# Attention outputs leave one step later: copies and adds moved behind the next split in a hybrid encoder layer

## The chip, the cores and the metric

The kernel runs on one core of one Trainium2 chip. The metric is the device time in microseconds of one launch, as the median of several runs; lower is better. The core has five engines with a queue each: TensorE (PE, with its weight loads as PEld), VectorE (DVE), ScalarE (ACT), GpSimd (POOL) and SyncE (SP), which only issues transfers here. An engine takes the instructions of its queue in order. Engines meet through semaphores.

## The reference

One layer over 1024 tokens of 1024 features, all in float32:

```python
hn = rmsnorm(h, norm_mix)
proj = einsum('bsd,de->bse', hn, w_in)           # 2304 columns: qa, ka, va, qb, kb, vb
o_a = window_gqa_sink(qa, ka, va, sink)          # 8 heads, 2 key heads, |i-j| <= 128, rotary on 16 of 64 dims
o_b = neighbourhood_attention(qb, kb, vb, rpb)   # 8 heads on a 16 x 64 grid, window 8 x 16, learned bias
mix = concatenate([rmsnorm(o_a, norm_a), rmsnorm(o_b, norm_b)])
h = h + einsum('bse,ed->bsd', mix, w_out)
hn = rmsnorm(h, norm_ffn)
h = h + down(silu(conv3(gate(hn))) * up(hn))     # 2816 inner features
return rmsnorm(h, norm_final)
```

Both attentions are softmax(scores) times values; the first has one extra logit per head (the sink) in its denominator.

## The kernel before, in words

Features lie on the 128 partitions and tokens along the free dimension. Every float32 product is made of three matmuls in a reduced format: each operand is split into a high part (a rounded copy) and a low part (the rest), and high by high, low by high and high by low are accumulated. ScalarE makes the high part, VectorE subtracts to get the low one.

The kernel has three stages: the first projections, then attention interleaved with the other projections (about 60 to 350 us), then the gated MLP. The second stage matters here. It is a list of units. A window unit (`unit_window`) is one block of 128 queries of a group of four heads; a grid unit (`units_grid`) is a part of one head's eight blocks. A unit has two kinds of steps:

- a q step makes scores (PE L393), reduces and biases them on VectorE (L424), takes the exponential on ScalarE (L432) and, for a pair, the reciprocal of the sums on VectorE (L434) and the scaling on GpSimd (L436).
- a t step transposes the scaled probabilities into a PSUM bank `pt` (PE L472 for windows, L548 for the grid) and splits them in `split_pt`: the high part `ph` on ScalarE (L446), the low part `pl` on VectorE (L447). The marks "high" and "rest" name the latest of these two. The t step returns a v step.
- a v step multiplies values with `ph` and `pl` into the output bank `o` (PE L478 and L479, grid L559 and L560). It is issued one t step later, so that the split has time.

When the last v step of a unit (of a half head on the grid) has been issued, `leave` takes the output out of `o`. The output lies in two halves of partitions, one product with the high and one with the low half of the values, and they have to be added across partitions: ScalarE copies one half into `ot` (L491, grid L574), VectorE adds the other half and writes it to `mix` (L495, grid L576). There is one `ot` buffer and there are two `o` banks.

Between these steps a generator (`rest`) fills TensorE with the remaining projections, three matmuls at a time (L179, L180, L181) into one of two banks `pj`, at rates set by the table `RATES`. The last of these jobs (`OutA`) are the first half of the output projection; each adds its bank to the residual on VectorE (L659) and so frees it. Projections of queries, keys and values leave their bank at L242 or L247.

TensorE's order is the order in which the code is written. On the other engines a scheduler sets the order by priority (`tc.high_priority`) and dependences. `behind(*names)` puts what is traced inside it behind the marked instructions of the same engine's queue; it orders the queue and adds no wait on a semaphore. The page's names are those of the code: `s` scores, `nm` the negated maximum, `sm` the sums, `xr` the residual's input, `raw`, `whi` and `wlo` a weight and its parts.

Of the kernel before, what the change touches and what calls it, by code (L numbers as in the profile page):

```python
# [58 lines left out]
def hybrid_layer(tc, xT, w_first, w_in, w_out, w_gate, w_up, w_down, small, sink, rpb, consts, rope, out):  # L59
    nc = tc.nc  # L60
    with ExitStack() as ctx:
# [13 lines left out]
        def big(name, tag, dt=F32):  # L75
            return lpool.tile([128, S], dt, name=name, tag=tag, bufs=slots[tag])
# [77 lines left out]
        def behind(*names):  # L154

            stack = ExitStack()
            for n in names:
                stack.enter_context(tc.issue_after(mark[n].ins))
            return stack
# [242 lines left out]
                return lpool.tile([128, 2, 386], F32, name="p", tag="mix", bufs=slots["mix"], padded_shape=[128, 2, 512])  # L402
            return apool.tile([128, 2, 386], F32, name="p", tag="p", bufs=5, padded_shape=[128, 2, 392])

        deferred = []

        def exponentials(*order):
            while deferred:
                with tc.high_priority(offset=50):
                    deferred.pop(0)(*order)  # L410
# [31 lines left out]
        def split_pt(ps, n):  # L442
            ph = apool.tile([128, HALF], F32R, name="ph", tag="ph")
            pl = apool.tile([128, HALF], F32R, name="pl", tag="pl")
            with tc.high_priority(offset=100):
                mark["high"] = nc.scalar.activation(ph[:, 0:n], ps[:, 0:n], AF.Copy)  # L446
                mark["rest"] = nc.vector.tensor_tensor(pl[:, 0:n], ps[:, 0:n], f32(ph[:, 0:n]), op=ALU.subtract)  # L447
            return ph, pl

        def unit_window(g, b):  # L450

            cs, n = near(b), 128 * len(near(b))
            ps4 = [None] * 4
            mask = w2(cst[:, K_MA + 128 * (cs[0] - b + 1):K_MA + 128 * (cs[-1] - b + 2)])
            st = {}

            def q_step(j):
                def go():
                    if j % 2 == 0:
                        st["p"] = pair_tile(True)  # L460
                    ps, _ = scores(qa[g, j // 2][j % 2], ka[g], b)
                    softmax(st, j % 2, ps, n, mask, nsink[:, 4 * g + j - j % 2:4 * g + j - j % 2 + 2])
                    ps4[j] = st["p"][:, j % 2, :]
                return go

            def t_step(i):
                def go():
                    if i == 0:
                        st["o"] = bank("o", "o")
                    pt = bank("pt", "pt")  # L470
                    for j in range(4):
                        nc.tensor.transpose(pt[:, j * 128:(j + 1) * 128], ps4[j][:, i * 128:(i + 1) * 128], ident)  # L472
                    ph, pl = split_pt(pt, HALF)
                    exponentials("high")

                    def v_step():
                        o, v = st["o"], va[g]
                        nc.tensor.matmul(o, v[:, cs[i], :], mv(ph[:, :]), start=i == 0, stop=False)  # L478
                        nc.tensor.matmul(o, v[:, cs[i], :], mv(pl[:, :]), start=False, stop=i == len(cs) - 1)  # L479
                        if i == len(cs) - 1:  # L480
                            leave()
                    return v_step
                return go

            def leave():
                ot = apool.tile([128, 2, 128], F32, name="ot", tag="ot", bufs=1, padded_shape=[128, 4, 128])
                o4 = pv(st["o"][:, :])
                halved = lambda ap: ap.rearrange("p (s w) -> p s w", s=2)
                for e in range(2):
                    me, other = slice(64 * e, 64 * e + 64), slice(64 - 64 * e, 128 - 64 * e)  # L490
                    nc.scalar.activation(ot[me].rearrange("p j (s w) -> p j s w", s=2), o4[other, e::2], AF.Copy)  # L491
                    for i in range(2):
                        if mix[2 * g + i] is None:
                            mix[2 * g + i] = big("mixa", "mix")
                        nc.vector.tensor_tensor(halved(mix[2 * g + i][me, b * 128:(b + 1) * 128]), o4[me, e + 2 * i], halved(ot[me, i, :]), op=ALU.add)  # L495

            return [q_step(j) for j in range(4)], [t_step(i) for i in range(len(cs))]

# [19 lines left out]
        def units_grid(h):  # L518

            ps4 = [None] * NB  # L520
            st = {"begun": [False, False]}
            e = 64 * (h % 2)
            me, other = slice(e, e + 64), slice(64 - e, 128 - e)

            def q_step(b):
                def go():
                    if b == 0:
                        bias_of[h] = bias_of.pop(h, None) or bias_tiles(h)
                    if b == 4 and h < 7:
                        bias_of[h + 1] = bias_tiles(h + 1)  # L530
                    x = bias_of[h]
                    if b % 2 == 0:
                        st["p"] = pair_tile()
                    sel = slice(2, 5, 2) if b == 0 else slice(0, 3, 2) if b == NB - 1 else slice(1, 4)
                    ps, n = scores(qb[h], kb[h], b)
                    softmax(st, b % 2, ps, n, x[:, sel, :] if n == 256 else w2(x[:, sel, :].rearrange("p c w -> p (c w)")))
                    ps4[b] = st["p"][:, b % 2, :]
                return go

            def t_step(c):  # L540
                def go():
                    if c == 0:
                        st["o"] = [bank("o", "o") for _ in range(2)]
                    bs = near(c)
                    pt = bank("pt", "pt")
                    for i, b in enumerate(bs):
                        at = near(b).index(c) * 128
                        nc.tensor.transpose(pt[:, i * 128:(i + 1) * 128], ps4[b][:, at:at + 128], ident)  # L548
                    ph, pl = split_pt(pt, 128 * len(bs))

                    def v_step():
                        for half in range(2):
                            inb = [b for b in bs if b // 4 == half]
                            if not inb:
                                continue
                            lo, hi = (inb[0] - bs[0]) * 128, (inb[-1] - bs[0] + 1) * 128
                            dst = st["o"][half][:, (inb[0] % 4) * 128:(inb[-1] % 4 + 1) * 128]
                            final = c == (4 if half == 0 else NB - 1)
                            nc.tensor.matmul(dst, vb[h][:, c, :], mv(ph[:, lo:hi]), start=not st["begun"][half], stop=False, skip_group_check=True)  # L559
                            nc.tensor.matmul(dst, vb[h][:, c, :], mv(pl[:, lo:hi]), start=False, stop=final, skip_group_check=True)  # L560
                            st["begun"][half] = True
                            if final:
                                leave(half)
                    return v_step
                return go

            def leave(half):
                i = 4 + h // 2
                if mix[i] is None:
                    mix[i] = big("mixb", "mix")  # L570
                ot = apool.tile([128, HALF], F32, name="ot", tag="ot", bufs=1)
                w = lambda ap: ap.rearrange("p (b r c s) -> p b s r c", s=2, r=ROWS // 2, c=8)
                o = st["o"][half]
                nc.scalar.activation(ot[me], o[other], AF.Copy)  # L574
                dst = mix[i][me, :].rearrange("p (s r b c) -> p b s r c", s=2, b=NB, c=8)[:, 4 * half:4 * half + 4]
                nc.vector.tensor_tensor(dst, w(o[me, :]), w(ot[me, :]), op=ALU.add)  # L576

            chunks = [[0], [1, 2], [3, 4], [5, 6, 7]]
            return [([q_step(2 * i), q_step(2 * i + 1)], [t_step(c) for c in chunks[i]]) for i in range(4)]
# [56 lines left out]
        class OutA:  # L636
# [12 lines left out]
            def run(self):  # L649
                d = self.d  # L650
                h1[d] = big("h1", "mix" if d < 4 else "op")
                xt = tmp("xr")
                with behind(*["stacked"] * (d > 0)):
                    nc.sync.dma_start(xt, xT[d])
                for h in range(2):
                    ps = bank("pj", "pj")
                    yield from product(ps, self.w, mg[0:4], h)
                    with tc.high_priority(offset=500):
                        nc.vector.tensor_tensor(sv(h1[d][:, tsl(h)]), pv(ps[:, :]), sv(xt[:, tsl(h)]), op=ALU.add)  # L659

            def post(self):
# [304 lines left out]
            nc.scalar.activation(warm, eps, AF.Sqrt)  # L966
        fill(2)
        pend()


        last = tmp("sq")
# [712 lines left out]
```

## Time and profile before

| | us |
|---|---|
| median of 3 runs | 1016.34 |
| lowest and highest run | 1015.89, 1016.55 |
| the profiled execution, whole | 1016.91 |
| its span, first to last instruction | 1015.1 |
| TensorE busy | 1006.3 |
| VectorE busy | 832.7 |
| ScalarE busy | 561.8 |
| GpSimd busy | 104.0 |

In the rows of the timeline the first number is the start in us from the start of the span, the second the time to the end of the row's last instruction, then engine, line, operation, what is written and read, the shape, and how many instructions the row merges; a bracket gives the idle time of the engine before it and what ended it. In the list of waits the numbers are the total in us, how many waits, and the longest. A matmul's end is modelled, and matmuls overlap; what TensorE loses at a place is read from the distances between starts. A row of the instruction order has the line, the operation, what is written and read with buffer numbers, and the shape; it has no time in it.

### The profile page before, as it was taken

To read this page: it belongs to the slowest core of one execution; us is meant where nothing else is said; L and a number is where in the kernel's file an instruction comes from. 1 tells how busy PE (TensorE), PEld (TensorE's weight loads), DVE (VectorE), ACT (ScalarE), POOL (GpSimd) and SP (SyncE) were. 2 spreads that over 40 slices of the span, in tenths; PEclk is the share of its full clock that TensorE was granted. 3 is DMA by queue.
4 is the path that set the end of the run, shared out by engine and by line. 5 is a ranking of instruction groups with operands and counts; after the bars stand their busy time and mean duration, and the time that the engine had idled before them with its cause. 6 is when DMAs were issued, how large, how long until landed. Compare 5 with 4: busy or idle time off the path is not lost.

```text
span 1015.1 us, 14835 instructions
## 1 busy us (share of the span) xinstructions
PE 1006.3 (99%) x5086; PEld 890.2 (88%) x5086; DVE 832.7 (82%) x1566; ACT 561.8 (55%) x1081; POOL 104.0 (10%) x188
## 2 busy tenths in 40 slices
PE   9999999999999999999999999999999999999996
PEld 8899898899899888888888888888888888888886
DVE  7989887768888799999987786786777678986775
ACT  8567776658687554565544443444443645544451
POOL 0224342222232100000000000000000000000002
PEclk9999999999999999999999999999999999999999
DMA  8223122333334366231542233323232699866644
GB/s 295 83 74 92 34 73 63 83 83 83 84 93 135 126 203 222 73 104 63 203 180 100 98 115 114 104 94 131 88 135 88 227 345 322 297 226 231 226 153 166
DMA packets 68220, 144.94 MB, mean 143 GB/s; under 512 B 8240, under 2 KB 18736, under 8 KB 68144
## 3 DMA queue, kind: packets, MB, share of 16 engines
q1 hardware_dynamic: 58208, 118.88, 36.5%
q10 hardware_dynamic: 9936, 25.11, 6.4%
q8 instruction: 40, 0.66, 0.3%
q14 instruction: 36, 0.29, 0.1%
HBM read 103.58 MB, written 28.57 MB: 130 GB/s over the span
## 4 chain that ended last, share of the span: by engine, by line
PE 99%; DVE 1%; issue 0%; ACT 0%; DVEq 0%; POOL 0%; POOLq 0%
PE pj L179 8%; PE pj L181 8%; PE pj L180 8%; PE x L1045 7%; PE x L1043 7%; PE x L1044 7%; PE dn L1045 7%; PE dn L1044 7%; PE dn L1043 7%; PE s L393 4%; PE y L1045 4%; PE y L1043 4%; PE y L1044 4%; PE pt L472 2%; PE z L1043 2%; PE z L1045 2%
## 5 line engine op out<-in xcount | busy, mean ns | idle before, releaser
L1043 PE MATMUL x<-hg,whi 128*128 128x512 f32 x352 | 133.5, 379 | 0.0
L1044 PE MATMUL x<-hg,whi 128*128 128x512 f32 x352 | 133.4, 379 | 0.0
L1045 PE MATMUL x<-hg,wlo 128*128 128x512 f32 x352 | 133.4, 379 | 0.0
L1043 PE MATMUL dn<-xd,whi 128*128 128x512 f32 (+1 forms) x330 | 120.8, 366 | 0.0
L1044 PE MATMUL dn<-xd,whi 128*128 128x512 f32 (+1 forms) x330 | 120.5, 365 | 0.0
L1045 PE MATMUL dn<-xd,wlo 128*128 128x512 f32 (+1 forms) x330 | 120.5, 365 | 0.0
L1017 ACT ACTIVATE whi<-ws 128x512 fp32r<-128x512 f32 (+1 forms) x100 | 60.7, 621 | 74.1 <-DVE ws L1153 14.7
L432 ACT ACTIVATE p<-p,nm 128x385 f32<-128x385 f32 (+3 forms) x128 | 75.1, 587 | 47.0 <-DVE nm L424 44.1
L179 PE MATMUL pj<-xgh,whi 128*128 128x512 f32 x245 | 99.7, 407 | 0.1
L436 POOL TENSOR_SCALAR p<-p,sm 128x384 f32<-128x384 f32 (+1 forms) x128 | 75.6, 603 | 196.0 <-DVE sm L434 179.9
L180 PE MATMUL pj<-xgl,whi 128*128 128x512 f32 x245 | 92.9, 379 | 0.0
L181 PE MATMUL pj<-xgh,wlo 128*128 128x512 f32 x245 | 92.9, 379 | 0.0
L1017 ACT ACTIVATE whi<-raw 128x512 fp32r<-128x512 f32 (+1 forms) x102 | 60.9, 610 | 50.1 <-PE x L1044 15.4
L1018 DVE TENSOR_TENSOR wlo<-ws,whi 128x512 fp32r<-128x512 f32 (+1 forms) x100 | 66.7, 683 | 19.1 <-ACT whi L1017 18.8
L447 DVE TENSOR_TENSOR pl<-pt,ph 128x384 fp32r<-128x384 f32 (+2 forms) x108 | 63.3, 586 | 17.4 <-ACT ph L446 16.3
L1043 PEld LDWEIGHTS x<-hg,whi 128*128 128x128 f32 x352 | 66.5, 189 | 9.5
L1045 PEld LDWEIGHTS x<-hg,wlo 128*128 128x128 f32 x352 | 66.5, 189 | 9.4
L1044 PEld LDWEIGHTS x<-hg,whi 128*128 128x128 f32 x352 | 66.5, 189 | 9.4
L1504 POOL TENSOR_TENSOR h<-h,wide 128x256 f32<-128x256 f32 (+1 forms) x6 | 5.4, 916 | 669.8 <-ACT wide L1500 669.8
L1018 DVE TENSOR_TENSOR wlo<-raw,whi 128x512 fp32r<-128x512 f32 (+1 forms) x102 | 66.7, 670 | 7.0 <-ACT whi L1017 6.8
L446 ACT ACTIVATE ph<-pt 128x384 fp32r<-128x384 f32 (+2 forms) x108 | 55.3, 512 | 25.8 <-PE pt L472 14.4
L1045 PEld LDWEIGHTS dn<-xd,wlo 128*128 128x128 f32 x330 | 62.5, 189 | 7.7
(267 smaller groups left out, 2507.6 us busy)
## 6 DMA issues: line engine op xcount, KB each, us to landing
xd<-x SPq DMA_DIRECT2D x77, 256.0 KB, 4.9
raw<-in_w_down_dram SPq DMA_DIRECT2D x72, 256.0 KB, 4.5
raw<-in_w_gate_dram SPq DMA_DIRECT2D x22, 512.0 KB, 3.5
raw<-in_w_up_dram SPq DMA_DIRECT2D x22, 512.0 KB, 3.7
x<-c ACTq DMA_DIRECT2D x22, 512.0 KB, 2.8
raw<-in_w_in_dram SPq DMA_DIRECT2D x30, 256.0 KB, 2.7
raw<-in_w_down_dram SPq DMA_DIRECT2D x36, 192.0 KB, 4.4
x<-t ACTq DMA_DIRECT2D x11, 512.0 KB, 2.6
```

Of the source, the lines that this page charges most:

```text
L179: nc.tensor.matmul(ps, w[0], mv(x[0][:, tsl(h)]), start=first, stop=False)
L180: nc.tensor.matmul(ps, w[0], mv(x[1][:, tsl(h)]), start=False, stop=False)
L181: nc.tensor.matmul(ps, w[1], mv(x[0][:, tsl(h)]), start=False, stop=last)
L432: nc.scalar.activation(p[:, j, 0:e], p[:, j, 0:e], AF.Exp, bias=nm, scale=-1.0, accum_out=sm[:, j:j + 1])
L436: mark["scaled"] = nc.gpsimd.tensor_scalar(p[:, i, 0:m], p[:, i, 0:m], sm[:, i:i + 1], 1.0, op0=ALU.mult, op1=ALU.mult)
L446: mark["high"] = nc.scalar.activation(ph[:, 0:n], ps[:, 0:n], AF.Copy)
L447: mark["rest"] = nc.vector.tensor_tensor(pl[:, 0:n], ps[:, 0:n], f32(ph[:, 0:n]), op=ALU.subtract)
L1017: nc.scalar.activation(hi, src, AF.Copy)
L1018: nc.vector.tensor_tensor(lo, src, f32(hi[:, :, :]), op=ALU.subtract)
L1043: nc.tensor.matmul(ps, w[0], x[0], start=first and i == 0, stop=False, skip_group_check=True)
L1044: nc.tensor.matmul(ps, w[0], x[1], start=False, stop=False, skip_group_check=True)
L1045: nc.tensor.matmul(ps, w[1], x[0], start=False, stop=last and i == len(ws) - 1, skip_group_check=True)
```

## The change

Three edits, all in the second stage:

- `leave` is no longer called in the last v step. It is put on a list `leaving`, and the next t step calls it (`leave_all`) after its own split has been issued, behind "high" on ScalarE and behind "rest" on VectorE. So the copy stands behind the next high part and the add behind the next low part. A last `leave_all()` stands after the last v step.
- the `mix` tiles are allocated ahead of the copy and not between the adds.
- the addition of an output projection (L659) stands behind the latest low part.

```diff
-        deferred = []
+        deferred, leaving = [], []
+
+        def leave_all(*order):
+            while leaving:
+                leaving.pop(0)(order)
...
                     ph, pl = split_pt(pt, HALF)
                     exponentials("high")
+                    leave_all("high", "rest")
...
                         if i == len(cs) - 1:
-                            leave()
+                            leaving.append(leave)
...
-            def leave():
+            def leave(order):
...
-                for e in range(2):
-                    me, other = slice(64 * e, 64 * e + 64), slice(64 - 64 * e, 128 - 64 * e)
-                    nc.scalar.activation(ot[me].rearrange("p j (s w) -> p j s w", s=2), o4[other, e::2], AF.Copy)
-                    for i in range(2):
-                        if mix[2 * g + i] is None:
-                            mix[2 * g + i] = big("mixa", "mix")
-                        nc.vector.tensor_tensor(halved(mix[2 * g + i][me, b * 128:(b + 1) * 128]), o4[me, e + 2 * i], halved(ot[me, i, :]), op=ALU.add)
+                for i in range(2):
+                    if mix[2 * g + i] is None:
+                        mix[2 * g + i] = big("mixa", "mix")
+                with behind(*order):
+                    for e in range(2):
+                        me, other = slice(64 * e, 64 * e + 64), slice(64 - 64 * e, 128 - 64 * e)
+                        nc.scalar.activation(ot[me].rearrange("p j (s w) -> p j s w", s=2), o4[other, e::2], AF.Copy)
+                        for i in range(2):
+                            nc.vector.tensor_tensor(halved(mix[2 * g + i][me, b * 128:(b + 1) * 128]), o4[me, e + 2 * i], halved(ot[me, i, :]), op=ALU.add)
...
                     ph, pl = split_pt(pt, 128 * len(bs))
+                    leave_all("high", "rest")
...
                             if final:
-                                leave(half)
+                                leaving.append(lambda order, half=half: leave(half, order))
...
-            def leave(half):
+            def leave(half, order):
...
-                nc.scalar.activation(ot[me], o[other], AF.Copy)
                 dst = mix[i][me, :].rearrange("p (s r b c) -> p b s r c", s=2, b=NB, c=8)[:, 4 * half:4 * half + 4]
-                nc.vector.tensor_tensor(dst, w(o[me, :]), w(ot[me, :]), op=ALU.add)
+                with behind(*order):
+                    nc.scalar.activation(ot[me], o[other], AF.Copy)
+                    nc.vector.tensor_tensor(dst, w(o[me, :]), w(ot[me, :]), op=ALU.add)
...
-                    with tc.high_priority(offset=500):
+                    with tc.high_priority(offset=500), behind("rest"):
                         nc.vector.tensor_tensor(sv(h1[d][:, tsl(h)]), pv(ps[:, :]), sv(xt[:, tsl(h)]), op=ALU.add)
...
         pend()
+        leave_all()
```

## The prediction

> **What bounds the kernel now.** I read the page first, then TensorE's waits by releaser, then start times on its timeline where it waits. The page:
>
> ```profile
> span 1015.1 us, 14835 instructions
> ...
> PE 1006.3 (99%) x5086; PEld 890.2 (88%) x5086; DVE 832.7 (82%) x1566; ACT 561.8 (55%) x1081; POOL 104.0 (10%) x188
> ...
> PE 99%; DVE 1%; issue 0%; ACT 0%; DVEq 0%; POOL 0%; POOLq 0%
> ```
>
> TensorE is busy in 99% of the span and is 99% of the chain that ended last. Nothing on VectorE (82%) or ScalarE (55%) shortens the kernel unless TensorE waits for it. The changed code runs between 60 and 350 us; this is everything TensorE's weight loads wait for from 40 to 400 us:
>
> ```profile
> PEld o L560 <- DVE pl L447: 0.5, 2, 0.3
> PEld s L393 <- DVE nm L424: 0.3, 1, 0.3
> PEld o L479 <- DVE pl L447: 0.3, 1, 0.3
> PEld pj L179 <- DVE v L206: 0.2, 1, 0.2
> PEld pj L179 <- PE pj L181: 0.2, 1, 0.2
> ```
>
> Six waits, 1.5 us in all: that bounds any gain at 0.15% of the span. About 0.2% is what a measurement of this kernel can tell from no change (2.0 us). Three of the six (0.8 us) are for `pl`, the low part of a split, which the change moves forward.
>
> **The change, part by part.** No instruction is added or removed, and TensorE's order is word for word the same. The new edges (`issue_after`) order queues and add no semaphore wait. What moves is the order on VectorE and ScalarE, and a little on GpSimd and SP. In the changed program line numbers are higher: L447 is L451, L424 L428, L432 L436, L434 L438, L446 L450, L574 L584, L576 L585, L659 L668.
>
> *Relief, third grid wait (333 us).* ScalarE before:
>
> ```order
> L446 ACTIVATE ph_4254<-pt_4251 128x256
> L171 ACTIVATE whi_4261<-raw_4259 128x512
> L574 ACTIVATE ot_4285<-o_4004 64x512
> L432 ACTIVATE p_4272,sm_4277<-p_4272,nm_4276 128x384
> L446 ACTIVATE ph_4292<-pt_4288 128x384
> ```
>
> and after:
>
> ```order
> L450 ACTIVATE ph_4254<-pt_4251 128x256
> L171 ACTIVATE whi_4261<-raw_4259 128x512
> L450 ACTIVATE ph_4289<-pt_4285 128x384
> L436 ACTIVATE p_4272,sm_4277<-p_4272,nm_4276 128x384
> L584 ACTIVATE ot_4293<-o_4004 64x512
> ```
>
> The copy `ot` and an exponential fall behind the high part. VectorE at the same place before:
>
> ```order
> L172 TENSOR_TENSOR wlo_4262<-raw_4259,whi_4261 128x512
> L576 TENSOR_TENSOR mixb_4188<-o_4004,ot_4285 64x4x16x8
> L424 ISA p_4272,nm_4302<-s_4299,xb_3958 128x256
> L424 ISA nm_4302 128x1
> L447 TENSOR_TENSOR pl_4293<-pt_4288,ph_4292 128x384
> ```
>
> and after:
>
> ```order
> L172 TENSOR_TENSOR wlo_4262<-raw_4259,whi_4261 128x512
> L451 TENSOR_TENSOR pl_4290<-pt_4285,ph_4289 128x384
> L428 ISA p_4272,nm_4302<-s_4299,xb_3958 128x256
> L428 ISA nm_4302 128x1
> L585 TENSOR_TENSOR mixb_4198<-o_4004,ot_4293 64x4x16x8
> ```
>
> The low part now stands ahead of the add and of a score reduction. The timelines there:
>
> ```profile
> 333.43 0.33 PE L559 MATMUL o<-ph,v 128*128 128x384 f32 x1
> 333.75 0.43 PE L560 MATMUL o<-pl,v 128*128 128x384 f32 x1
> 334.02 0.38 PE L179 MATMUL pj<-mgh,whi 128*128 128x512 f32 x1
> ...
> 331.58 0.68 DVE L172 TENSOR_TENSOR wlo<-raw,whi 128x512 fp32r<-128x512 f32 x1
> 332.19 0.70 DVE L576 TENSOR_TENSOR mixb<-o,ot 64x512 f32<-64x512 f32 x1
> 333.16 0.54 DVE L447 TENSOR_TENSOR pl<-pt,ph 128x384 fp32r<-128x384 f32 x1
> 333.63 0.67 DVE L659 TENSOR_TENSOR h<-pj,xr 128x512 f32<-128x512 f32 x1
> ...
> 331.14 0.59 ACT L574 ACTIVATE ot<-o 64x512 f32<-64x512 f32 x1
> 332.42 0.49 ACT L446 ACTIVATE ph<-pt 128x384 fp32r<-128x384 f32 x1
> ```
>
> `pl` ended at 333.70 and TensorE started on it at 333.75. After, the high part can start where the copy did (331.14, end 331.63) and `pl` behind `wlo` (332.19 to 332.73), 0.9 us before TensorE wants it. The wait goes. Its price from starts: 333.43 to 333.75 is 0.32 and 333.75 to 334.02 is 0.27, where an undisturbed matmul of 384 columns takes 0.17 (next fence, 279.04 to 279.21): 0.15 + 0.10 = 0.25 us. The second 0.10 is the restart behind a wait.
>
> *The other two waits for `pl`:*
>
> ```profile
> 279.04 0.33 PE L559 MATMUL o<-ph,v 128*128 128x384 f32 x1
> 279.21 0.43 PE L560 MATMUL o<-pl,v 128*128 128x384 f32 x1
> 279.48 0.49 PE L548 MATMUL pt<-cst,p 128*128 128x128 f32 x3
> ...
> 277.43 0.79 DVE L576 TENSOR_TENSOR mixb<-o,ot 64x512 f32<-64x512 f32 x1
> 278.61 0.55 DVE L447 TENSOR_TENSOR pl<-pt,ph 128x384 fp32r<-128x384 f32 x1
> ...
> 106.41 0.48 PE L479 MATMUL o<-pl,v 128*128 128x512 f32 x1
> 106.73 0.49 PE L472 MATMUL pt<-cst,p 128*128 128x128 f32 x3
> ...
> 104.53 0.50 DVE L495 TENSOR_TENSOR mixa<-o,ot 64x128 f32<-64x128 f32 x2 [0.34 <-ACT ot L491]
> 105.67 0.68 DVE L447 TENSOR_TENSOR pl<-pt,ph 128x512 fp32r<-128x512 f32 x1
> ```
>
> At 279 the add of 0.79 us moves behind `pl`; TensorE lost 0.27 - 0.17 = 0.10. At 106 the pair of adds (0.50, and 0.34 idle for its copy) moves behind; 0.32 less 0.22 (0.17 by 512 over 384 columns) = 0.10. Relief together 0.25 + 0.10 + 0.10 = 0.45 us. Bounds: 0, if something else turns late; 1.5, if all six waits go. I take 0.45: these rows name the moved work, the others do not. (By the list of waits these three are worth 0.8, by the starts 0.45; a weight load is queued ahead of its matmul, so part of its wait lies beside the matmul before it, and the starts decide.) What is late next at 333 is the high part itself, wanted by TensorE at 333.43 and then ready at 331.63.
>
> *What a copy that leaves later holds up.* A copy at the head of ScalarE's queue that waits for TensorE's last product holds every split and exponential behind it. Behind the next high part it finds its product long finished, since the transposes that this high part reads stand after that product in TensorE's order. On VectorE the add still waits for its copy, and what is queued behind it, mostly the next score reduction, is moved back by no more than the add itself, 0.70 to 0.79 in the rows above. The last add of the stage is still issued straight after the last product, so the norm that follows the stage starts as before. Cost 0.
>
> *What stays.* The wait at 257 is for a reduction:
>
> ```profile
> 256.94 0.48 PE L179 MATMUL pj<-xgh,whi 128*128 128x512 f32 x1
> ...
> 256.22 0.67 DVE L206 TENSOR_REDUCE v<-ss 128x4 f32<-128x512 f32 x1
> ```
>
> An add slides there from ahead of one half of a key split to ahead of the other, still ahead of the reduction: no gain, no loss.
>
> *Projection additions (L659) go later.* VectorE at 326 us, before:
>
> ```order
> L434 RECIPROCAL sm_4153<-sm_4153 128x2
> L576 TENSOR_TENSOR mixb_4188<-o_4003,ot_4189 64x4x16x8
> L659 TENSOR_TENSOR h1_4141<-pj_4144,xr_4142 128x512
> L447 TENSOR_TENSOR pl_4199<-pt_4194,ph_4198 128x384
> L424 ISA p_4207,nm_4211<-s_4208,xb_3958 128x384
> ```
>
> and after:
>
> ```order
> L438 RECIPROCAL sm_4153<-sm_4153 128x2
> L451 TENSOR_TENSOR pl_4195<-pt_4190,ph_4194 128x384
> L585 TENSOR_TENSOR mixb_4198<-o_4003,ot_4199 64x4x16x8
> L668 TENSOR_TENSOR h1_4141<-pj_4144,xr_4142 128x512
> L428 ISA p_4207,nm_4211<-s_4208,xb_3958 128x384
> ```
>
> The addition frees a `pj` bank (two buffers) and stands one low part later. Three additions, and the matmuls that reuse their banks:
>
> ```profile
> 326.56 0.67 DVE L659 TENSOR_TENSOR h<-pj,xr 128x512 f32<-128x512 f32 x1
> 327.17 0.53 DVE L447 TENSOR_TENSOR pl<-pt,ph 128x384 fp32r<-128x384 f32 x1
> 329.51 0.67 DVE L659 TENSOR_TENSOR h<-pj,xr 128x512 f32<-128x512 f32 x1
> ...
> 328.46 0.46 PE L179 MATMUL pj<-mgh,whi 128*128 128x512 f32 x1
> 332.70 0.46 PE L179 MATMUL pj<-mgh,whi 128*128 128x512 f32 x1
> 336.87 0.46 PE L179 MATMUL pj<-mgh,whi 128*128 128x512 f32 x1
> ```
>
> The first ends at 327.23, 1.23 before 328.46; behind `pl` (0.53) 0.70 is left. The second ends at 330.18, 2.52 ahead of 332.70; 1.21 more work stands ahead of it, which leaves 1.31. The third (the 333.63 row) ends at 334.30, 2.57 ahead of 336.87; with 0.68 more, 1.89 is left. So the forecast cost is 0; if that cover goes, TensorE waits the overrun plus a 0.10 restart. The `o` banks are two as well, and a bank is wanted again a unit later; the add falls back by less than a step of transposes (328.46 to 332.70 are two steps, so one is 2.1).
>
> The Trainium skill's Perfetto Trace Analysis, section Matmuls, speaks against this part: groups should rotate through PSUM banks so that one group's evacuation overlaps the next group's matmuls, and a later evacuation gives some of that overlap up. By that rule the time is that of the slower rival below; by the rows just shown 0.70 us of overlap is left at the tightest place.
>
> *GpSimd and SP.*
>
> ```profile
> 132.58 0.42 POOL L423 COPY p<-nsink 128x2 f32<-128x2 f32 x3
> 134.39 1.14 POOL L436 TENSOR_SCALAR p<-p,sm 128x384 f32<-128x384 f32 x2 [1.40 <-DVE sm L434]
> 136.74 0.60 ACT L446 ACTIVATE ph<-pt 128x512 fp32r<-128x512 f32 x1 [1.12 <-PE pt L472]
> ...
> 307.85 0.58 SPq L164 DMA_DIRECT2D raw<-in_w_out_dram  x1
> 309.12 3.46 SPq L654 DMA_DIRECT2D xr<-in_xT_dram  x2
> 320.10 0.62 ACT L171 ACTIVATE whi<-raw 128x512 fp32r<-128x512 f32 x1
> ```
>
> Three sink copies move behind the next scaling pair, to about 135.6. An exponential that ran at 134.9 wants the first and may be 0.8 late; ScalarE then idled 1.12 for TensorE, which covers it. One weight load moves behind two transfers, to about 309.5, 1.6 later; its reader runs at 320.1. Both cost 0; without cover, 0.8 and 1.6 at most.
>
> **Sum.** The profiled execution took 1016.91 us (span 1015.1, 1.8 around it); less 0.45 that is 1016.5. It stands 0.57 above the median of 1016.34, so the forecast for a median is 1016.34 - 0.45 = 1015.9.
>
> **Rivals.** (1) Nothing arrives: the waits for `pl` are followed by others and TensorE stays as it is, 1016.3. For it: six waits are few, and what comes first on a shared queue makes something else second. Against it: the three rows name moved work and leave 0.9 us at 333. (2) All six waits go, because queues that wait less run ahead: 1016.34 - 1.5 = 1014.8. Against it: the reduction at 257 keeps its place. (3) Slower: additions miss their bank. It decides once the low part they are tied to comes more than 0.70 late. If each slides by a whole step of 2.1, the three places overrun by 1.4, 0.8 and 0.2, with three restarts 2.7 us: 1015.9 + 2.7 = 1018.6. Against it: `pl` itself runs earlier almost everywhere.
>
> **How the numbers follow.** Forecast 0.62 (own range 1015.3 to 1016.5, the runs of before spread over 0.66), rival 1 0.16, rival 2 0.09, rival 3 0.08, unseen 0.05. The range 1014.7 to 1017.3 holds the first three and part of rival 3's smaller overruns. By the 0.2% bound the first three are all "same", with a little of rival 2 beyond it: faster 0.03, same 0.88, slower 0.09 (rival 3 and unseen).
>
> **What would show it.** Right: no wait for `pl` (L451) in TensorE's list of waits, starts 0.17 apart at the three places, the reduction's wait still there. Wrong: a wait of `pj` for the projection additions, of `o` for the adds, or more than 1.5 us in TensorE's waits in that stretch.

## The result, and the profile after

The changed kernel takes 1017.64 us (median of 21 runs, 1017.12 to 1018.16), the kernel before 1016.34 in the same session (21 runs, 1015.44 to 1016.89). The ratio is 1.0013, with a 95% interval of 1.0007 to 1.0018: slower, by 0.7 to 1.8 us. That is inside the 0.2% that I called no change, but it lies outside my range, and on the other side of the kernel before than my forecast. The profiled execution took 1017.44 us. Of all the runs told below, two executions took about 1520 us at a granted TensorE clock of 0.654 (one of e1_one_back, the one traced, and one of e3_additions_alone); they are left out, and e1_again gives e1's trace.

The page of the changed kernel:

```profile
span 1015.7 us, 14829 instructions
...
PE 1004.8 (99%) x5086; PEld 889.2 (88%) x5086; DVE 833.1 (82%) x1566; ACT 561.7 (55%) x1081; POOL 105.0 (10%) x188
...
PE 94%; DVE 2%; ACT 2%; DMA 1%; issue 1%; SPq 0%; POOL 0%; DVEq 0%
```

TensorE's busy time fell by 1.5 us and the span rose by 0.6, so TensorE waits about 2 us more. The chain that ended last leaves TensorE in the changed stage between 238 and 258 us and runs there through VectorE, ScalarE and GpSimd. What TensorE's weight loads wait for from 40 to 400 us in the changed kernel:

```profile
PEld pj L179 <- DVE v L206: 1.9, 1, 1.9
PEld s L393 <- DVE nm L428: 0.2, 1, 0.2
PEld o L568 <- DVE pl L451: 0.2, 1, 0.2
```

Six waits became three. The three waits for `pl` that I counted on are gone; the one for `pl` in this list is at another place, 336 us, and costs 0.08 us there. At the third of those three places the changed kernel's TensorE starts its matmuls 0.16 us apart, as an undisturbed one does:

```profile
334.23 0.33 PE L567 MATMUL o<-ph,v 128*128 128x384 f32 x1
334.39 0.33 PE L568 MATMUL o<-pl,v 128*128 128x384 f32 x1
334.55 0.38 PE L179 MATMUL pj<-mgh,whi 128*128 128x512 f32 x1
```

No projection addition (L668) and no output bank is in the list. But the one wait whose place I had called "no gain, no loss" went from 0.2 to 1.9 us. It is the wait for the second reduction of the norm that follows the window attention (L206); the timelines of the changed kernel there:

```profile
256.14 0.28 PE L393 MATMUL s<-kb,q 128*128 128x256 f32 x1
258.07 0.48 PE L179 MATMUL pj<-xgh,whi 128*128 128x512 f32 x1 [1.66 <-DVE v L206]
258.39 0.38 PE L180 MATMUL pj<-xgl,whi 128*128 128x512 f32 x1
...
253.53 1.03 DVE L303 SCALAR_TENSOR_TENSOR kb<-t,cst,ka 128x512 fp32r<-128x512 f32 x1
255.29 0.78 DVE L585 TENSOR_TENSOR mixb<-o,ot 64x512 f32<-64x512 f32 x1
256.00 1.42 DVE L303 SCALAR_TENSOR_TENSOR kb<-t,cst,ka 128x512 fp32r<-128x512 f32 x1
257.35 0.67 DVE L206 TENSOR_REDUCE v<-ss 128x4 f32<-128x512 f32 x1
...
252.59 1.43 POOL L440 TENSOR_SCALAR p<-p,sm 128x384 f32<-128x384 f32 x2 [5.67 <-DVE sm L438]
255.45 1.42 POOL L519 TENSOR_TENSOR xb<-cst,rr 128x384 f32<-128x384 f32 x1 [1.43 <-DVE nm L428]
```

TensorE's starts are 1.93 us apart where 0.11 is usual behind a matmul of 256 columns, and 0.32 for the next where 0.22 is usual: 1.93 us lost in all (0.32 in the trace shown before the prediction). The reader should see two things on VectorE. The add (L585) stands ahead of the second half of a key split (L303). And the two halves, the same instruction on the same shape, take 1.03 and 1.42 us, where before they took 0.73 and 0.74:

```profile
254.08 0.73 DVE L303 SCALAR_TENSOR_TENSOR kb<-t,cst,ka 128x512 fp32r<-128x512 f32 x1
255.55 0.74 DVE L303 SCALAR_TENSOR_TENSOR kb<-t,cst,ka 128x512 fp32r<-128x512 f32 x1
```

Each of the long ones runs while GpSimd works: the first beside a scaling (L440), the second beside the building of a bias tile (L519).

### The profile page after: what moved, and what is told of

Same layout as the page of the kernel before. It is cut to its first block, busy times and chain, and to the rows that moved or that the text cites. A ratio compares the mean times of both kernels' runs of the same rounds, so it can differ in the third digit from the quotient of the medians.

```text
span 1015.7 us, 14829 instructions
## 1 busy us (share of the span) xinstructions
PE 1004.8 (99%) x5086; PEld 889.2 (88%) x5086; DVE 833.1 (82%) x1566; ACT 561.7 (55%) x1081; POOL 105.0 (10%) x188
## 4 chain that ended last, share of the span: by engine, by line
PE 94%; DVE 2%; ACT 2%; DMA 1%; issue 1%; SPq 0%; POOL 0%; DVEq 0%
PE pj L179 8%; PE x L1053 7%; PE x L1054 7%; PE x L1055 7%; PE pj L181 7%; PE pj L180 7%; PE dn L1055 7%; PE dn L1053 7%; PE dn L1054 7%; PE y L1054 4%; PE y L1053 4%; PE y L1055 4%; PE s L393 4%; PE pt L476 2%; PE z L1053 2%; PE z L1054 2%
## 5 line engine op out<-in xcount | busy, mean ns | idle before, releaser
L440 POOL TENSOR_SCALAR p<-p,sm 128x384 f32<-128x384 f32 (+1 forms) x128 | 76.9, 613 | 198.7 <-DVE sm L438 177.6
L451 DVE TENSOR_TENSOR pl<-pt,ph 128x384 fp32r<-128x384 f32 (+2 forms) x108 | 63.5, 588 | 20.9 <-ACT ph L450 19.5
L1384 ACT ACTIVATE xd<-xd 128x512 fp32r<-128x512 f32 x77 | 47.4, 625 | 43.4 <-DMA xd<-x 43.2
L1054 PEld LDWEIGHTS dn<-xd,whi 128*128 128x128 f32 x330 | 62.5, 189 | 7.7
```

The source lines that it names most:

```text
L440: mark["scaled"] = nc.gpsimd.tensor_scalar(p[:, i, 0:m], p[:, i, 0:m], sm[:, i:i + 1], 1.0, op0=ALU.mult, op1=ALU.mult)
L1054: nc.tensor.matmul(ps, w[0], x[1], start=False, stop=False, skip_group_check=True)
L1384: nc.scalar.activation(hi, f32(lo), AF.Copy)
```

## The experiments

Below, "lost" is a distance between two TensorE starts less the usual one (0.11, 0.16 and 0.22 us behind 256, 384 and 512 columns), with the restart that follows (0.10, at 274 us 0.07). "Stage" is the time from the first score matmul to the last transposes of probabilities, which leaves out the start of the kernel and the MLP. Each timed kernel had its own runs of the kernel before in the same session; "against before" is the difference of the two medians. The intervals of these ratios are about 0.0009 to either side, 0.9 us, so for most of these kernels the time alone settles nothing, and the traces do. "Elsewhere" leaves out two places where every row loses about 0.1: 277 us and 182 us (there up to 0.07 more in the changed kernel than before).

| kernel | against before, us | stage, us | lost at 256 us | at 274 | at 333 | elsewhere |
|---|---|---|---|---|---|---|
| before, first trace | | 289.7 | 0.32 | 0.21 | 0.26 | 0.41 (103, 106, 279 us) |
| before_again | | 289.3 | 0.25 | 0.21 | 0.26 | 0.09 (279) |
| the change | +1.30 | 290.5 | 1.93 | 0 | 0 | 0.08 (336) |
| after_again | | 290.4 | 1.93 | 0 | 0 | |
| e1_one_back, e1_again | +0.08, +0.46 | 289.4 | 0.90 | 0 | 0 | |
| e2_one_moved | +0.40 | 289.5 | 0.50 | 0.18 | 0.23 | 0.06 (279) |
| e3_additions_alone | +0.19 | 289.4 | 0.20 | 0.21 | 0.52 | 0.06 (279) |
| e4_no_additions | +1.89 | 291.0 | 1.97 | 0 | 0.53 | |
| e5_tile_held | +0.96 | 290.2 | 1.27 | 0.32 | 0 | 0.10 (336) |
| e6_one_later | +0.16 | 289.5 | 0.74 | 0.25 | 0 | |
| e12_early_later_held | +1.19 | 290.3 | 0 | 1.02 | 0 | 0.57 (253), 0.10 (336) |
| e14_no_tile | +1.35 | 290.5 | 1.93 | 0 | 0 | 0.08 (336) |
| e15_no_tile_there | +2.84 | 291.7 | 1.22 | 0 | 0 | 1.99 (296) |

Two columns carry the reading. Taking the second trace of before (289.3) as the base, the stage differs by what the time differs, to within 0.4 us in every row; and the lost starts, summed, differ by what the stage differs, to within 0.15. So the whole loss is in this stage, and it is made of these few waits.

### The traces once more

`before_again` and `after_again` are the two kernels without an edit.

> The kernel before, once more, for a second trace. If its first trace was a typical execution (theory A1): the same six waits, TensorE's lost starts at 103, 106, 256, 274, 279 and 333 us, and 289.7 us from its first score matmul to its last transposes of probabilities. If some of these waits belong to that one execution (theory A2, since the kernel with the additions alone has the same orders up to 290 us and shows no lost start at 103 and 106 and 0.10 instead of 0.33 at 256): those three are gone or small, and the stretch takes 289.1 to 289.4 us.

> The changed kernel, once more, for a second trace. Theory A: TensorE's lost start at 256 us is there again with 1.8 to 1.95 us, with the second half of the key split at 1.4 us, and the stretch from the first score matmul to the last transposes takes 290.4 to 290.6 us. If that wait belonged to one execution: less than 1.2 us, and less than 290.0 us.

The waits in the second trace of the kernel before (1016.09 us, stage 289.3):

```profile
PEld o L560 <- DVE pl L447: 0.5, 2, 0.3
PEld pj L179 <- PE pj L181: 0.2, 1, 0.2
PEld pj L179 <- DVE v L206: 0.2, 1, 0.2
```

The lost starts at 103 and 106 us (0.31 in all) are not in it; those at 256, 274 and 333 are, and so is the one at 279 (starts at 277.96, 278.12 and 278.37, the second of the two waits of L560 in the list). The first trace, on which the forecast was built, was of an execution 0.57 us above its median, and about that much longer in this stage. In the changed kernel the wait is in both traces with the same 1.93 us, and in those of two more kernels that keep its order at this place (e4 1.97, e14 1.93). It belongs to the order, not to an execution.

### One copy and add put back, and the same one moved alone

```diff
                             if final:
-                                leaving.append(lambda order, half=half: leave(half, order))
+                                if (h, half) == (2, 1):
+                                    leave(half, ())
+                                else:
+                                    leaving.append(lambda order, half=half: leave(half, order))
```

is e1 (and e1_again). e2 is its opposite: the kernel before, with this one place moved behind the next split and everything else as it was.

> The changed kernel, with the copy and add of one place alone (head 2, second half, the add at 255.29 us of the changed kernel's profile) issued straight after the last product again. Theory A (stretch): the loss is TensorE's one wait for the second norm reduction (256.14 to 258.07 us), and that came because the two halves of a key split on VectorE (L303) moved beside GpSimd's work and took 1.03 and 1.42 us where they took 0.73 and 0.74. The work ahead of the reduction is the same in either order, so what counts is where the halves fall: the add is ahead of both here, both halves stand behind the score reduction that also releases GpSimd's bias tile; I expect the reduction 0.25 to 1.1 us earlier and 1016.5 to 1017.4 us. Theory B (spread): the loss is not this wait, which takes slack that is lost elsewhere anyhow (later projection additions, later sink copies): 1017.6 us, unchanged. Theory C (plain order, no stretch): the same work stands ahead of the reduction, so the wait stays as it is: 1017.6 us with a wait of 1.9 us.

> The kernel with the one copy and add put back straight after the last product (head 2, second half), once more, for its trace. Theory A (the reduction comes late because the halves of the key split are stretched beside GpSimd): 1016.6 us again, TensorE's wait for the second norm reduction at 256 us 0.7 to 1.1 us instead of 1.9, and both halves together no more than 1.9 us (2.45 in the changed kernel). Theory C (plain order): a wait of 1.9 us still, and the microsecond gained elsewhere.

> The kernel before, with that one copy and add (head 2, second half) moved behind the next split, and nothing else of the change. Theory A (stretch): the reduction starts 0.7 to 1.1 us later than in the kernel before, TensorE's wait at 257 us grows by as much, and the time is 1017.0 to 1017.5 us. Theory B (spread): within 0.2 us of the kernel before, 1016.3. Theory C (plain order): 1016.3 too, as the work ahead of the reduction is the same.

VectorE, GpSimd and TensorE in e1_again:

```profile
254.94 1.40 DVE L303 SCALAR_TENSOR_TENSOR kb<-t,cst,ka 128x512 fp32r<-128x512 f32 x2
256.27 0.67 DVE L206 TENSOR_REDUCE v<-ss 128x4 f32<-128x512 f32 x1
...
255.10 2.08 POOL L519 TENSOR_TENSOR xb<-cst,rr 128x384 f32<-128x384 f32 x1 [1.12 <-DVE nm L428]
...
256.99 0.48 PE L179 MATMUL pj<-xgh,whi 128*128 128x512 f32 x1 [0.63 <-DVE v L206]
```

One of sixteen grid places put back recovers 1.03 of the 1.93 us, and with it most of the loss. The add is ahead of the reduction here too, as in the changed kernel; what differs is that the first half now starts before the bias tile and the second follows it without a gap, that they take 1.40 together instead of 2.45, and that the tile takes 2.08 us instead of 1.42. The half that starts first keeps its pace, and so does the one right behind it (0.73, though it starts 0.50 behind the tile's start); the tile pays. That is theory A, and plain order (theory C) is out.

e2 missed its number: I had 1017.0 to 1017.5 and it came to 1016.86. The same move at the same place costs only 0.25 us at 256 us there, since in this order both halves fall ahead of the low part:

```profile
252.83 1.69 DVE L303 SCALAR_TENSOR_TENSOR kb<-t,cst,ka 128x512 fp32r<-128x512 f32 x2
254.45 0.55 DVE L451 TENSOR_TENSOR pl<-pt,ph 128x384 fp32r<-128x384 f32 x1
...
255.42 0.98 POOL L519 TENSOR_TENSOR xb<-cst,rr 128x384 f32<-128x384 f32 x1 [2.09 <-DVE nm L428]
```

No half meets the bias tile. The first meets a scaling (252.75 to 253.33) and takes 1.03 of the 1.69, 0.30 more than alone, and that is about what TensorE loses here. The tile, with only the add beside it, takes 0.98 us: that is its own length. So the move alone is not the cause; it is the move together with where the halves then fall. What is lost in e1 (0.65 above before) and in e2 (0.25) do not add up to the 1.68 of the whole change.

### Where the other 0.65 us comes from

In e1 TensorE still loses 0.90 against 0.25 in before_again. From the first of the two reductions to the second it is 3.39 us in e1_again and 3.41 in before_again, so the rest is lost ahead of the first. The first can start once its transposes (L205) are done. In before_again:

```profile
250.27 0.60 PE L205 MATMUL ss<-cst,sq 128*128 128x128 f32 x4
...
243.71 0.79 DVE L576 TENSOR_TENSOR mixb<-o,ot 64x512 f32<-64x512 f32 x1
251.67 0.68 DVE L206 TENSOR_REDUCE v<-ss 128x4 f32<-128x512 f32 x1
```

and in after_again:

```profile
250.41 0.60 PE L205 MATMUL ss<-cst,sq 128*128 128x128 f32 x4
...
244.10 0.17 DVE L438 RECIPROCAL sm<-sm 128x2 f32<-128x2 f32 x1 [0.17 <-ACT p L436]
244.62 1.53 DVE L196 TENSOR_TENSOR sq<-sq 128x512 f32<-128x512 f32 x2 [0.36 <-ACT sq L194]
247.02 0.78 DVE L585 TENSOR_TENSOR mixb<-o,ot 64x512 f32<-64x512 f32 x1
252.53 0.68 DVE L206 TENSOR_REDUCE v<-ss 128x4 f32<-128x512 f32 x1
...
244.43 2.10 POOL L440 TENSOR_SCALAR p<-p,sm 128x384 f32<-128x384 f32 x2 [5.67 <-DVE sm L438]
```

From the start of the transposes to the reduction it is 1.40 us before and 2.12 after (2.12 in e1_again too): 0.72 later, measured from TensorE. The add of the same head's first half was at 243.71, where VectorE had nothing else to do: in the changed kernel it idles there for 0.17 and 0.36 us, for ScalarE. The add then takes its 0.78 at 247.02, where VectorE is behind. The idle 0.53 is most of the 0.72. Another 0.25 is a third stretch: the first of the two sums of squares at 244.62 (L196, two inputs in SBUF) starts 0.19 behind a scaling of GpSimd and takes 0.93 of the 1.53, where in before_again it started 0.24 ahead of that scaling and took 0.68. This part was read from the rows; that one place was not put back alone.

### GpSimd's tile taken away from the second half

```diff
-            with behind(*["scaled"] * (h == 7)):
+            with behind(*["scaled"] * (h in (5, 7))):
```

is e5: head 5's bias tile waits in GpSimd's queue behind a later pair of scalings. VectorE's, ScalarE's and TensorE's orders are word for word those of the changed kernel.

> The changed kernel, with the bias tile of head 5 (two GpSimd operations, L519 and L520, at 255.45 to 257.99 us) issued behind a later pair of scalings on GpSimd; the orders of TensorE, VectorE and ScalarE stay word for word. Theory A (stretch): the second half of the key split falls from 1.42 to about 0.74 us, the first stays at 1.03 (beside a scaling), the reduction starts 0.68 us earlier: 1016.9 to 1017.0 us. Theory B (spread) and theory C (plain order): the half takes what it took, 1017.6 us.

VectorE and GpSimd in e5:

```profile
255.75 0.73 DVE L303 SCALAR_TENSOR_TENSOR kb<-t,cst,ka 128x512 fp32r<-128x512 f32 x1
272.03 1.06 DVE L864 SCALAR_TENSOR_TENSOR mixa<-mixa,par,rstda 128x512 f32<-128x512 f32 x1
...
271.56 0.99 POOL L519 TENSOR_TENSOR xb<-cst,rr 128x384 f32<-128x384 f32 x1
272.49 1.19 POOL L520 TENSOR_TENSOR xb<-cst,rr 128x256 f32<-128x256 f32 x1
```

Nothing but GpSimd's work was moved, and the half fell from 1.42 to 0.73; the wait fell by 0.66. This shows that GpSimd's tile stretches the half and that TensorE pays for it. The time missed its number (1017.42 for 1016.9 to 1017.0), because the tile met another VectorE instruction where it went: a norm scaling (L864) takes 1.06 instead of 0.75, and TensorE now loses 0.32 at 274 us (nothing in the changed kernel), and 0.10 at 336.

Two more kernels tried to take the tile away without a place to collide in. Head 5 uses head 4's tile:

```diff
-                        bias_of[h + 1] = bias_tiles(h + 1)
+                        bias_of[h + 1] = bias_of[h] if h == 4 else bias_tiles(h + 1)
```

(e14), and e15 is the same with `h == 7` made `h >= 6` in the line of e5.

> The changed kernel without head 5's bias tile: the tile of head 4 is used for both heads, so the two GpSimd operations at 255.45 us and their load are left out. What this leaves out is head 5's own bias, so its output is another. Theory A (VectorE's half waits for GpSimd): the second half of the key split takes 0.74 instead of 1.42 us, TensorE's lost start at 256 us falls from 1.83 to about 1.15, and, as no tile collides with a norm scaling at 272 us either, no new wait comes there: 1017.6 - 0.7 = 1016.9 us. If GpSimd has nothing to do with it (theory C): 1.4 us for the half, and 1017.6 us.

> The run without head 5's tile left a tile at 255 us after all: head 6's, which needs only the same buffer, moved up into its place, and the wait was the same. Here that one is held as well, behind the scalings of head 5, so that GpSimd is idle from the scalings at 252 to those at 258 us and no tile stands at 272 us. Left out, as before, is head 5's own bias (head 4's is used), so the output is another. Theory A (VectorE's half of the key split waits for GpSimd): the half 0.74 us instead of 1.42, TensorE's lost start at 256 us 1.15 instead of 1.83, none or under 0.3 at 274, and 1016.8 to 1017.1 us. Theory C (GpSimd has nothing to do with it): 1.4 us for the half and 1017.6 us.

e14 didn't test what it was to test: the tile of head 6, which waits for the same buffer, moved up into the free place, and the half took 1.40 as ever. In e15 the place is free at last. The half takes 0.71, TensorE loses 1.22 instead of 1.93, and nothing at 274. But the kernel is the slowest of all, for another reason. TensorE's waits and SP's queue in e15:

```profile
PEld s L393 <- DVE mixb L585: 1.1, 1, 1.1
PEld s L393 <- DMA kb<-ka: 0.9, 1, 0.9
...
SPq L510 <- POOL xb L520: 2.5, 1, 2.5
```

The held tile keeps its raw buffer, the next load of such a buffer (L510) waits for it at the head of SP's queue, and the transfers of a key (`ka<-kb`, `kb<-ka`) stand behind it in that queue; the scores at 296 us lose 1.99. The list puts the second of their two waits down to such a transfer and the first to an add (L585), so how much of the 1.99 the transfers cost is not shown. So what the stretch of the second half costs at its place is measured twice, 0.66 and 0.71 us; I have no kernel that gets this back as time.

### The add moved past the reduction, and the wait taken away whole

e6 keeps that one copy and add for one more step of transposes:

```diff
         def leave_all(*order):
+            if leaving and keep[0]:
+                keep[0] -= 1
+                return
             while leaving:
...
                                 leaving.append(lambda order, half=half: leave(half, order))
+                                if (h, half) == (2, 1):
+                                    keep[0] = 1
```

e12 adds to this the held tile of e5, and puts the second reduction's transposes one step of the projection earlier, its root staying behind the next high part:

```diff
-        aux[11, 8], aux[12, 2], aux[12, 5], aux[12, 11], aux[12, 13] = square_a, narrow_a, narrow_a, wide_a(0), wide_a(1)
+        aux[11, 8], aux[12, 2], aux[12, 4], aux[12, 11], aux[12, 13] = square_a, narrow_a, narrow_a, wide_a(0), wide_a(1)
+        aux[12, 6] = root_a
```

> The changed kernel, with that one copy and add (head 2, second half) kept for one step of transposes more, so that the add (0.78 us) stands behind the second norm reduction. Theory A (stretch): the reduction comes 0.78 us earlier for the add, and up to 0.68 more if the half of the key split, now right behind the score reduction, starts before GpSimd's bias tile does: 1016.2 to 1016.9 us. Theory B (spread): 1017.6 us. Theory C (plain order): 0.78 us less, 1016.9 us, with both halves as long as before the change.

> The changed kernel with the whole wait at 256 us taken away: the transposes of the second norm reduction one step of the projection earlier (its square root stays behind the next high part), the one copy and add (head 2, second half) a step later still, head 5's bias tile behind a later pair of scalings. The reduction should stand right behind the score reduction (about 255.3 us), end before TensorE wants its bank, and the half of the key split take 0.74. Theory A (that wait is the loss, less what a small wait at 274 us takes back): 1017.6 - 1.9 + 0.2 = 1015.9 us, against 1016.3 to 1016.5 of the kernel before. Theory B (spread): 1017.0 us or more.

e6 came as expected: without the add in between, the half starts 0.16 us ahead of the tile and takes 0.74, the reduction follows, and TensorE loses 0.74. e12 missed by 1.6 us (1017.46 for 1015.9). Its wait at 256 us is gone, but two others came. TensorE's waits in e12:

```profile
PEld pj L179 <- PE s L393: 1.1, 1, 1.1
PEld ss L205 <- DVE v L206: 0.6, 1, 0.6
```

The earlier transposes want the bank of the first reduction before VectorE has freed it (0.57 at 253 us), and at 274 TensorE, now earlier, wants a bank that VectorE frees at 275.00 in e12 and at 275.50 in the changed kernel, where TensorE wants it only at 275.72. From 267 to 275 us VectorE has no gap of more than 0.04 us. Of the loss at 274, about 0.27 comes from the held tile, as in e5: it meets a norm scaling, which takes 1.02 instead of 0.75. Of the 1.93 that TensorE wins at 256 it loses 1.02 there and 0.57 at 253: this stretch is VectorE's, and one wait can't be priced alone.

### The projection additions

e3 is the kernel before with `behind("rest")` on the additions and nothing else, e4 the changed kernel without it.

> The kernel before, with the projection additions (L658 here) issued behind the latest low part, and no other part of the change. Theory A: their cover of 0.70 us and more holds, TensorE has no wait for these additions, and the time is that of the kernel before, 1016.2 to 1016.7 us. Theory B (the loss, or a part of it, lies in the later additions): 1016.9 us or more, with waits of the projection's bank between 325 and 345 us.

> The changed kernel without its part on the projection additions: the attention outputs leave a step later, the additions are issued as before. Theory A: the wait at 256 us stays 1.9 us, and the time is that of the changed kernel, 1017.3 to 1017.8 us. Theory B: 1016.3 to 1017.0 us.

Neither has a wait for an addition. TensorE at the third grid wait, in e3 and then in e4:

```profile
332.75 0.42 PE L559 MATMUL o<-ph,v 128*128 128x384 f32 x1
333.33 0.43 PE L560 MATMUL o<-pl,v 128*128 128x384 f32 x1 [0.16 <-DVE pl L447]
```

```profile
334.04 0.43 PE L567 MATMUL o<-ph,v 128*128 128x384 f32 x1
334.63 0.43 PE L568 MATMUL o<-pl,v 128*128 128x384 f32 x1 [0.16 <-DVE pl L451]
```

With one part alone, either part, TensorE loses 0.52 or 0.53 there, twice the 0.26 of before; with both, nothing. No addition's bank is waited for, but moved alone the additions make this low part 0.26 late: in e3 one of them runs at 330.27 us, ahead of the reduction, the weight's low part and the add that stand before this low part. In e4 it is the high part (L450) that comes late: it ends at 333.99 us. The relief at 333 us needs both edits. e4 came 0.4 us above its range, and these 0.53 us, which I had not put into it, are why.

No kernel here beats both: the best (e1, e3, e6) are at the time of the kernel before.

## Why the prediction was wrong

- *The relief* (three waits for `pl`, 0.45 us): these waits went. But the 0.10 at 106 us was a wait of the one execution that I had read; the second trace doesn't have it. What the order itself lost was 0.26 at 333, 0.25 at 256, 0.21 at 274 and 0.09 at 279, and the change took all but the one at 256 away: 0.56. The 0.21 at 274 I had not named, so that the size came out near is in part luck. The cover at 333 was too large: `pl` ends at 334.17 there, 0.22 us ahead of TensorE's start at 334.39 and not 0.9, since an addition (L668, 331.95 us) now stands ahead of it.
- *Additions later, cost 0*: right, and for the reason given: no addition missed its bank. That the additions, moved alone, make a low part late (0.26 in e3) was not in it.
- *GpSimd and SP reordered, cost 0*: right for what I looked at, the sink copies and the loads. What I did not look at is what GpSimd does beside VectorE.
- *What stays* is the step that failed: "An add slides there from ahead of one half of a key split to ahead of the other, still ahead of the reduction: no gain, no loss." I counted the instructions ahead of the reduction, found the same ones, and took their durations as fixed. The same instructions took 0.30 and 0.68 us more, because the slide put both halves behind the start of a GpSimd instruction. And the work did not start at the same time: "moved back by no more than the add itself, 0.70 to 0.79", priced at 0 a paragraph earlier, was the right size, but at 244 us the add had filled a gap of VectorE's, and from there to the reduction VectorE has no gap in which to make it up: 0.72. Of that 0.72, 0.25 is again an instruction stretched beside GpSimd. Together 0.72 + 0.30 + 0.68 = 1.70, against 1.93 - 0.25 = 1.68 lost; the two stretches are taken against the first trace, and in before_again, where the halves took 0.77 and 0.80, the distance between the reductions is 3.41 against 4.42, which gives 0.72 + 1.01 = 1.73.
- *The sum*: 1.68 for this step instead of 0, less 0.56, is 1.12; with 0.07 more at 182 us and 0.08 at 336 it is 1.27. Measured: +1.30 (0.7 to 1.8), and 1.2 by the stages of the traces.
- *The rivals*: none named this place. The slower one put the loss at the additions, where there is none, and priced it at 2.7 us. My list of things that would prove me wrong had "more than 1.5 us in TensorE's waits", and that is what came (1.9 in one wait).

## What to carry to other kernels

When an instruction slides past others, the same list of instructions ahead of a wait is not the same time: look at what GpSimd runs beside each of VectorE's instructions, and who starts first. An add that fills a gap of its engine costs nothing there and its full length where the engine is behind. And waits of 0.1 to 0.3 us in a single trace may belong to that execution; take a second trace before they become terms of a sum.

## What the runs showed of the hardware

VectorE and GpSimd delay each other. In the rows above an instruction of VectorE that reads two tensors from SBUF began three times while a GpSimd instruction ran, and each ended 0.54 to 0.55 us after that one: in the changed kernel at 254.56 behind 254.02 and at 257.42 behind 256.87, in e5 at 273.09 behind 272.55. In the whole stage of the changed kernel's first trace (60 to 350 us) this happens 17 times: 13 of them end 0.53 to 0.55 us behind GpSimd's instruction; one began so late (180.46) that it kept its 0.67; in three (141.93, 149.95, 245.87) VectorE's instruction kept its length and GpSimd's was the long one, 1.24 to 1.53 us. The other way round, the bias tile (0.98 us alone, in e2) took 1.43 behind the start of one half (before) and 2.08 behind two (e1). VectorE's low parts (L451) and score reductions (L428), which read PSUM, show no such stretch: 0.53 to 0.55 and 0.40 to 0.41 us for 384 and 256 columns, with GpSimd busy or idle. The Trainium skill's SBUF — State Buffer, section SBUF: two separate sides, describes a port pair that the two engines share as an exclusive lock: whoever starts first has it for the whole instruction, and a VectorE operation with two SBUF inputs counts against a GpSimd operation that reads SBUF. The traces agree in the main. VectorE's instruction needs 0.54 us, not its whole 0.73, behind the end of GpSimd's, so about 0.2 of it lies ahead of the wait; and the tile of before, begun at 255.71 beside a half that ended at 256.29, ended at 257.14, where the rule with the tile's 0.98 gives 257.27. The three rows in which GpSimd's instruction began first by the trace and still was the long one don't follow from it as it stands. Nor does another: in the changed kernel the tile began 0.55 us ahead of the half and still took 1.42 instead of 0.98 (the same in after_again, e4 and e14), while in e5 it began 0.47 ahead of a norm scaling and took 0.99. Why is open.
